# Three held weight tiles over half of the feature blocks at a time, turned tiles in side banks, turned one tile sooner

## The chip, the cores and the metric

The kernel runs on one core of one Trainium2 chip. The metric is the device time of one execution in microseconds; the time before is the median of three runs. TensorE multiplies, ScalarE (ACT) casts and copies, VectorE (DVE) subtracts, adds and scales, and SyncE (SP) and GpSimd (POOL) issue most of the transfers.

## The reference

512 tokens of width 1024 pass through two layers. Each layer is a feed-forward block, a mixer and another feed-forward block, each behind a norm and added to the stream; a final norm ends it.

```python
x = x + 0.5 * swiglu(rms_norm(x, ffn1_norm[l]), ffn1_wg[l], ffn1_wu[l], ffn1_wd[l])
h = rms_norm(x, mix_norm[l])
z = h @ w_in[l]                      # q | k | v | conv B | conv C | conv h
...                                  # window attention, and B * causal conv3(C * h)
x = x + jnp.concatenate([attn_out, conv_out], axis=-1) @ w_out[l]
x = x + 0.5 * swiglu(rms_norm(x, ffn2_norm[l]), ffn2_wg[l], ffn2_wu[l], ffn2_wd[l])
```

`swiglu(h)` is `(silu(h @ w_gate) * (h @ w_up)) @ w_down` with 2816 hidden features; `rms_norm` divides each token by its root mean square and multiplies by a gain. All is float32.

## The kernel before

**Numbers in two parts.** A float32 operand is split into a high part, a cast by ScalarE (`wh`, L204), and a low part, the rest, by VectorE (`wl`, L205). Each product is three matmuls: high by high, high by low and low by high. Weights go through three buffers for high parts and three for low parts. `need_split(g)` makes the splits up to number g; a split waits until the matmuls on the tile that held its buffer are done.

**Large blocks.** Most of the feed-forward work runs in a seven-product scheme on forms of the activations: b11, b21, b22 and the sums t1 to t4, kept as `fb` and `ft` tiles. Their low parts too are subtractions of L205.

**The stage behind a norm.** The stream is kept with tokens on the partitions (four tiles t of 128 tokens, two halves o of 512 features). When two token tiles are complete, `Norm.stage` makes their factors (L569 to L571, and the Newton step at L452 to L454) and the normed tiles `xn` (L577). `Norm.pull` takes one token half and one feature half: `turn` transposes two `xn` tiles on TensorE (L601, four transposes of 128x128 each) into a PSUM tile `xt`, ScalarE casts it (L610), VectorE subtracts (L611), and in front of a feed-forward block ScalarE copies it once more in full (`hf`, L613), from which the sums are made (L634 to L640). A norm has four pulls: two for the first 256 tokens, two for the second. PSUM has eight banks: four with tag "mm", two "sc" and two "aux"; `Norm.tags` says which the turned tiles take.

**The block that opens behind the norm** is `halves` (five times in the kernel, called A to E in order of time, at 348, 512, 851, 1192 and 1356 us of the profiled span: A and D in front of the mixers, B, C and E in front of feed-forward blocks). It holds three weight tiles of 1024 x 128, and runs the first 256 tokens (`t` 0) for one tile after the other over all eight feature blocks `k`, then the second 256 tokens. The third and the fourth pull lie between, behind the second tile and in the middle of the third:

```python
for t in range(2):
    for j, (hi, lo) in enumerate(held):
        for k in range(KC):
            ...                                        # three matmuls of 256 columns (L317)
            if t == 0 and (j, k) in ((1, KC - 1), (2, KC // 2 - 1)):
                norm.pull()
        if t:
            need_split(first + j + 3)
            done(j, accs[j])
```

`done` is the caller's: in `plain_halves` it starts the gate (silu, L940) or the product with the third tile and makes the sums t2, t3 and t1. There a fourth tile (`up`, L952) follows, then the seven-product stages (L837); in the mixer a plain `group` (L291 to L294) follows.

**What runs ahead of it.** At A, B and E it is `share` (L837, evictions at L871), as the out projection or as the last shared stage of a feed-forward block: its seventh product has the first two pulls between its matmuls. At C and D it is `down` (L340, evictions at L1149): for its second half it holds three weight tiles, finishes token tiles 0 and 1 first, and then runs the three weights over token tiles 2 and 3; the pulls stand behind the last weight's matmuls of tile 2 and of tile 3.

**Order.** From the second half of `down`, or the fifth step of `share`, to the end of `halves`, TensorE's instructions stand in the order of the program (`by_hand`). VectorE's, ScalarE's and the rest are put in order by a scheduler when the kernel is built, from what depends on what.

Of the kernel before, what the change touches and what calls it, by code (L numbers as in the profile page):

```python
# [23 lines left out]
KC = D // P  # L24
# [3 lines left out]
H = S // 2  # L28
# [44 lines left out]
def trunk_kernel(  # L73
# [23 lines left out]
    nc = tc.nc  # L97
# [8 lines left out]
    def psum(tag, shape, name):  # L106
        return ps.tile(shape, F32, tag=tag, bufs={"mm": 4, "sc": 2, "aux": 2}[tag], name=name)
# [94 lines left out]

    def split(hi, lo, raw, eng=nc.vector):
        nc.scalar.copy(hi, raw)  # L204
        eng.tensor_sub(lo, raw, f32(hi))  # L205

    def split_far(hi, lo, raw):

        nc.scalar.activation(lo, raw, AF.Copy, scale=-1.0)
        nc.scalar.copy(hi, raw)  # L210
        return nc.gpsimd.dma_start(out=f32(lo), in_=raw, accum_op=ALU.add)

    def need_split(g):
        while state["split"] <= min(g, len(order) - 1):
            n = state["split"]
            u, what = order[n]
            far = what == "far"
            if what in (None, "wide", "far"):
                need_raw(u if far else u + LOAD_AHEAD)
                raw = raw_of.pop(u)  # L220
            elif isinstance(what, tuple):

                what, h, how = what
                far = how == "far"
                last = {"a11": 0, "a12": 4, "s2": 2, "s3": 6, "s1": 2, "a22": 8, "s4": 4}[what]
                need_raw(u + h if far else u + max(last, 4) + h + LOAD_AHEAD)
                a11, s1, a12, s3, a22 = (raw_of.get(u + 2 * i + h) for i in range(5))
                if what == "s2":
                    late = state["late"] if h else None
                    with tc.issue_after(late) if late else nullcontext():  # L230
                        nc.vector.tensor_add(a11, a11, s1)  # L231
                raw = {"a11": a11, "a12": a12, "s2": a11, "s3": s3, "s1": s1, "a22": a22, "s4": a12}[what]
            else:

                need_raw(u + 4 + LOAD_AHEAD)
                a11, a12, s1, s3, a22 = (raw_of.get(u + i) for i in range(5))
                if what == "s2":
                    nc.vector.tensor_add(a11, a11, s1)
                if what == "s4":
                    nc.vector.tensor_add(a11, a11, a12)  # L240
                raw = {"a11": a11, "a12": a12, "s2": a11, "s3": s3, "s1": s1, "a22": a22, "s4": a11}[what]
                if what == FORMS[-1]:
                    for i in range(5):
                        del raw_of[u + i]
            shape = list(raw.shape)
            hi = wpool.tile(shape, F32R, tag="wh", bufs=3, name=f"wh_{n}")
            lo = wpool.tile(shape, F32R, tag="wl", bufs=3, name=f"wl_{n}")
            if far:
                sent = split_far(hi, lo, raw)
            else:  # L250
                split(hi, lo, raw)
            if isinstance(order[n][1], tuple):
                early = how == "early"
# [12 lines left out]
                for i in done:  # L266
                    del raw_of[u + 2 * i + h]
            split_of[n] = (hi, lo)
            state["split"] += 1
            if far:  # L270

                with tc.issue_after(sent.ins):
                    need_raw(u + LOAD_AHEAD + (4 + h if isinstance(order[n][1], tuple) else 0))

    def take_split(ahead=SPLIT_AHEAD):
        n = state["group"]
        state["group"] += 1
        need_split(n + ahead)
        return n, *split_of.pop(n)
# [27 lines left out]
    def halves(norm, n, done):  # L307

        first = state["group"]
        held = [take_split(SPLIT_AHEAD - j)[1:] for j in range(n)]  # L310
        accs = [psum("mm", [P, S], f"acc_{first + j}") for j in range(n)]
        for t in range(2):
            for j, (hi, lo) in enumerate(held):
                for k in range(KC):
                    xh, xl = norm.half(k, t)
                    for i, (w, x_) in enumerate(((hi, xh), (hi, xl), (lo, xh))):
                        nc.tensor.matmul(  # L317
                            accs[j][:, t * H : (t + 1) * H],
                            w[:, k, :],
                            x_,  # L320
                            start=t + k + i == 0,
                            stop=k == KC - 1 and i == 2,
                            skip_group_check=True,
                        )
                    if t == 0 and (j, k) in ((1, KC - 1), (2, KC // 2 - 1)):
                        norm.pull()
                if t:
                    need_split(first + j + 3)
                    done(j, accs[j])

    def down(acts, blocks, norm=None):

        last = len(blocks) - 1

        def products(acc, t, i, wh, wl):
            tok = slice(t * P, (t + 1) * P)
            ah, al = acts[blocks[i]]
            for k in range(2):
                for n, (a, w) in enumerate(((ah, wh), (al, wh), (ah, wl))):
                    nc.tensor.matmul(  # L340
                        acc,
                        a[:, k, tok],
                        w[:, k, :],
                        start=i + k + n == 0,
                        stop=i == last and k == 1 and n == 2,
                    )

        for o in range(2):
            accs = [psum("mm", [P, S], f"down_{state['group']}_{t}") for t in range(NT)]
            if o and norm:  # L350
                by_hand()
            if o and last:
                held = [take_split(SPLIT_AHEAD - i)[1:] for i in range(last + 1)]
                ahead = state["group"]
                for t in range(2):
                    for i, w in enumerate(held):
                        products(accs[t], t, i, *w)
                    yield t, o, accs[t]
                for i, w in enumerate(held):
                    for t in range(2, NT):  # L360
                        products(accs[t], t, i, *w)
                        if i == last:
                            yield t, o, accs[t]
                            if norm:
                                norm.pull()
                    need_split(ahead + i)
                continue
            for i in range(last + 1):
                _, wh, wl = take_split()
                for t in range(NT):  # L370
                    products(accs[t], t, i, wh, wl)
                    if i == last:
                        yield t, o, accs[t]
# [283 lines left out]
    norm = First()  # L657
# [52 lines left out]
    def squares(n):  # L710
# [756 lines left out]
    def stages_of(i):  # L1467
        mixing = i % 3 == 1
        gain = (ffn1_norm, mix_norm, ffn2_norm)[i % 3][i // 3]
        late = ("sc", "sc", "aux", "aux") if mixing else ("mm", "mm", "sc", "sc")  # L1470
        return Norm(i, gain, mixing, ("aux", "aux", "sc", "sc") + late)

    for l in range(DEPTH):
        n1, n2 = stages_of(3 * l + 1), stages_of(3 * l + 2)
# [4 lines left out]
        norm = n3  # L1479
# [30 lines left out]
```

## Time and profile before

| | us |
|---|---|
| median of three runs | 1699.25 (1699.24 to 1699.68) |
| profiled execution | 1701.48 |
| its span | 1699.7 |
| TensorE busy | 1679.4 (99%) |
| VectorE busy | 1323.5 (78%) |
| ScalarE busy | 953.2 (56%) |
| mean granted TensorE clock | 0.996 |

The profiled execution has its own time: its span runs from the first to the last instruction, and 1.8 us lie around it. A timeline row has the start, the duration, the engine, the line, the operation, output <- inputs, the sizes and a count; in brackets stands how long the engine had been idle before it, and who released it. Durations of matmuls overlap, so that their starts, not their durations, tell the pace. A row of the windows has the stretch, busy time and instructions of each engine, the granted clock, the share of DMA time and GB/s.

### The profile page before, as it was taken

The numbers are of one execution on the slowest core, as the hardware profiler recorded it, in microseconds if no ns is written. First come the engines' busy times: TensorE is split into PE (matmuls) and PEld (weight loads), VectorE is DVE, ScalarE is ACT, GpSimd is POOL, SyncE is SP. The second block draws the span as 40 slices with busy tenths as digits, with TensorE's granted clock in tenths as the row PEclk, the third lists the DMA queues.
The fourth block names the chain that finished last, engine by engine and source line by source line (L and its number), as shares of the span: only waits on it lengthen the run. The fifth ranks groups of instructions, "written<-read, shape, count | busy, mean of one in ns | idle before, by whom it ended". The sixth has DMA issues, their size and how long they took to land.

```text
span 1699.7 us, 21898 instructions
## 1 busy us (share of the span) xinstructions
PE 1679.4 (99%) x8222; PEld 1412.8 (83%) x8222; DVE 1323.5 (78%) x1734; ACT 953.2 (56%) x1361; POOL 182.2 (11%) x164
## 2 busy tenths in 40 slices
PE   9999999999999999999999999999999999999998
PEld 6888898888888888888888888888888888888887
DVE  6987679867798766899577668995587986668993
ACT  6455565556566555555455555553565765556553
POOL 0011111000110111111001111110001101111101
PEclk9999999999999999999999999999999999999999
DMA  9367788721494777788537777883225947777971
GB/s 248 87 186 187 185 194 213 191 73 57 132 221 103 203 180 185 185 223 221 128 73 200 184 186 185 224 214 109 63 61 143 224 113 192 178 186 185 233 185 50
DMA packets 189310, 279.85 MB, mean 165 GB/s; under 512 B 8948, under 2 KB 73492, under 8 KB 189204
## 3 DMA queue, kind: packets, MB, share of 16 engines
q1 hardware_dynamic: 150900, 203.34, 38.5%
q0 software_dynamic: 37600, 74.46, 26.2%
q8 instruction: 64, 1.05, 0.2%
q10 hardware_dynamic: 704, 0.66, 0.1%
q14 instruction: 42, 0.34, 0.1%
HBM read 263.74 MB, written 2.10 MB: 156 GB/s over the span
## 4 chain that ended last, share of the span: by engine, by line
PE 94%; DVE 4%; ACT 1%; issue 0%; DMA 0%; SPq 0%; DVEq 0%; ACTq 0%
PE x L837 24%; PE y L837 12%; PE x_s L837 10%; PE w L837 6%; PE down L340 6%; PE y_s L837 5%; PE acc L317 4%; PE acc L291 4%; PE acc L292 4%; PE acc L294 4%; PE w_s L837 3%; PE at L1077 2%; PE x_m L837 2%; DVE wl L205 1%; PE up L952 1%; PE acc L735 1%
## 5 line engine op out<-in xcount | busy, mean ns | idle before, releaser
L204 ACT CAST wh<-raw 128x1024 fp32r<-128x1024 f32 (+1 forms) x494 | 516.3, 1046 | 563.4 <-PE x L837 126.4
L205 DVE TENSOR_TENSOR wl<-raw,wh 128x1024 fp32r<-128x1024 f32 (+1 forms) x494 | 597.6, 1212 | 243.0 <-ACT wh L204 241.2
L837 PE MATMUL x<-wh,ft 128*128 128x512 f32 x608 | 188.6, 391 | 0.0
L837 PE MATMUL y<-wh,ft 128*128 128x512 f32 x608 | 188.4, 391 | 0.0
L837 PE MATMUL x<-wh,fb 128*128 128x512 f32 x608 | 187.1, 389 | 0.0
L837 PEld LDWEIGHTS x<-wh,fb 128*128 128x128 f32 x608 | 113.9, 188 | 23.4
L837 PEld LDWEIGHTS x<-wh,ft 128*128 128x128 f32 x608 | 113.1, 188 | 22.8
L837 PEld LDWEIGHTS y<-wh,ft 128*128 128x128 f32 x608 | 113.1, 188 | 22.7
L837 PE MATMUL x<-wl,ft 128*128 128x512 f32 x304 | 118.3, 389 | 0.0
L837 PE MATMUL y<-wl,ft 128*128 128x512 f32 x304 | 118.3, 389 | 0.0
L837 PE MATMUL x<-wl,fb 128*128 128x512 f32 x304 | 118.3, 389 | 0.0
L199 POOL DMA_DIRECT2D raw<-in_ffn_wu_dram x39 | 47.2, 1210 | 539.6 <-DMA raw<-in_ffn_wu_dram 407.5
L837 PE MATMUL w<-wh,fb 128*128 128x512 f32 x304 | 95.2, 394 | 0.0
L291 PE MATMUL acc<-hh,wh 128*128 128x512 f32 x240 | 94.6, 394 | 0.0
L294 PE MATMUL acc<-hh,wl 128*128 128x512 f32 x240 | 93.9, 391 | 0.0
L292 PE MATMUL acc<-hl,wh 128*128 128x512 f32 x240 | 93.6, 390 | 0.0
L340 PE MATMUL down<-wh,a 128*128 128x512 f32 x288 | 89.2, 391 | 0.0
L837 PE MATMUL y_s<-wh,ft_s 128*128 128x512 f32 x256 | 79.5, 392 | 0.0
L837 PE MATMUL x_s<-wh,ft_s 128*128 128x512 f32 x256 | 79.2, 390 | 0.0
L199 POOL DMA_DIRECT2D raw<-in_ffn_wg_dram x39 | 47.0, 1213 | 265.6 <-DMA raw<-in_ffn_wu_dram 97.5
L837 PE MATMUL x_s<-wh,fb_s 128*128 128x512 f32 x240 | 74.2, 390 | 0.0
L231 DVE TENSOR_TENSOR raw<-raw,raw 128x1024 f32<-128x1024 f32 x58 | 70.5, 1219 | 0.5
(320 smaller groups left out, 3439.8 us busy)
## 6 DMA issues: line engine op xcount, KB each, us to landing
raw<-in_ffn_wu_dram SPq DMA_DIRECT2D x126, 512.0 KB, 3.8
raw<-in_ffn_wd_dram SPq DMA_DIRECT2D x104, 512.0 KB, 5.1
raw<-in_ffn_wg_dram SPq DMA_DIRECT2D x86, 512.0 KB, 5.0
raw<-in_ffn_wu_dram POOLq DMA_DIRECT2D x39, 512.0 KB, 7.5
raw<-in_ffn_wg_dram POOLq DMA_DIRECT2D x39, 512.0 KB, 6.0
raw<-in_w_in_dram SPq DMA_DIRECT2D x36, 512.0 KB, 3.9
raw<-in_ffn_wd_dram POOLq DMA_DIRECT2D x32, 512.0 KB, 7.8
raw<-raw POOLq DMA_DIRECT2D x20, 512.0 KB, 6.9
```

The source lines that it names most:

```text
L199: nc.gpsimd.dma_start(out=r, in_=rows_of(*more), accum_op=ALU.add)
L204: nc.scalar.copy(hi, raw)
L205: eng.tensor_sub(lo, raw, f32(hi))
L231: nc.vector.tensor_add(a11, a11, s1)
L291: nc.tensor.matmul(acc, hi[:, k, :], rhs[k][0], start=k == first, stop=False)
L292: nc.tensor.matmul(acc, hi[:, k, :], rhs[k][1], start=False, stop=False)
L294: nc.tensor.matmul(acc, lo[:, k, :], rhs[k][0], start=False, stop=k == last)
L317: nc.tensor.matmul(accs[j][:, t * H : (t + 1) * H], w[:, k, :], x_, start=t + k + i == 0, stop=k == KC - 1 and i == 2, skip_group_check=True,)
L340: nc.tensor.matmul(acc, a[:, k, tok], w[:, k, :], start=i + k + n == 0, stop=i == last and k == 1 and n == 2,)
L735: nc.tensor.matmul(opening[n], (lo if part == "w" else hi)[:, k, :], xl if part == "x" else xh, start=n not in begun, stop=k == KC - 1 and ...
L837: nc.tensor.matmul(accs[u], x_[:, 2 * h + k, tok], w[:, k, :], start=start and h + k + i == 0, stop=h + k == 2 and i == 2, skip_group_chec ...
L1077: nc.tensor.transpose(tp[:, t * P : (t + 1) * P], ups[t][:, c * P : (c + 1) * P], ident)
```

## The change

Three edits. `halves` takes the feature blocks in two fours: for each token half, the three held tiles run over the first four blocks, then all three over the other four; the third and the fourth pull stand behind the first and the second tile of the second four. `need_split` and `done` are called behind a tile's last four blocks. In `down`, the two pulls move from behind the last of the three weights to behind the last but one. And the turned tiles of the second token half take the side banks, "aux", "aux", "sc", "sc", as those of the first do, instead of "mm", "mm", "sc", "sc" (in front of a feed-forward block) or "sc", "sc", "aux", "aux" (in front of a mixer).

```diff
@@ halves @@
         for t in range(2):
-            for j, (hi, lo) in enumerate(held):
-                for k in range(KC):
-                    xh, xl = norm.half(k, t)
-                    for i, (w, x_) in enumerate(((hi, xh), (hi, xl), (lo, xh))):
-                        nc.tensor.matmul(
...
-                    if t == 0 and (j, k) in ((1, KC - 1), (2, KC // 2 - 1)):
+            for half in range(2):
+                for j, (hi, lo) in enumerate(held):
+                    for k in range(KC // 2 * half, KC // 2 * (half + 1)):
+                        xh, xl = norm.half(k, t)
+                        for i, (w, x_) in enumerate(((hi, xh), (hi, xl), (lo, xh))):
+                            nc.tensor.matmul(
...
+                    if not t and half and j < 2:
                         norm.pull()
-                if t:
-                    need_split(first + j + 3)
-                    done(j, accs[j])
+                    if t and half:
+                        need_split(first + j + 3)
+                        done(j, accs[j])
@@ down @@
                         if i == last:
                             yield t, o, accs[t]
-                            if norm:
-                                norm.pull()
+                        if norm and i + 1 == last:
+                            norm.pull()
@@ stages_of @@
-        late = ("sc", "sc", "aux", "aux") if mixing else ("mm", "mm", "sc", "sc")
-        return Norm(i, gain, mixing, ("aux", "aux", "sc", "sc") + late)
+        return Norm(i, gain, mixing, ("aux", "aux", "sc", "sc") * 2)
```

The changed program has the same matmuls, casts and subtractions; on TensorE they stand in the written order, and the scheduler's order of ScalarE and VectorE changes around C and D and behind each `halves`.

More of the change, by code (lines that the diff above doesn't have):

```diff
@@ L312, in halves @@
         for t in range(2):
-            for j, (hi, lo) in enumerate(held):
-                for k in range(KC):
-                    xh, xl = norm.half(k, t)
-                    for i, (w, x_) in enumerate(((hi, xh), (hi, xl), (lo, xh))):
[L317 to L324, printed above, removed]
-                    if t == 0 and (j, k) in ((1, KC - 1), (2, KC // 2 - 1)):
+            for half in range(2):
[4 more added lines that the diff above has]
+                            nc.tensor.matmul(
+                                accs[j][:, t * H : (t + 1) * H],
+                                w[:, k, :],
+                                x_,
+                                start=t + k + i == 0,
+                                stop=k == KC - 1 and i == 2,
+                                skip_group_check=True,
+                            )
+                    if not t and half and j < 2:
                         norm.pull()
-                if t:
-                    need_split(first + j + 3)
-                    done(j, accs[j])
+                    if t and half:
+                        need_split(first + j + 3)
+                        done(j, accs[j])
     def down(acts, blocks, norm=None):
```

## The prediction

> **What bounds the kernel now.** I read the page first, then TensorE's waits, then the chain, the timelines and the windows around the five places where a norm ends and `halves` begins.
>
> ```profile
> PE 1679.4 (99%) x8222; PEld 1412.8 (83%) x8222; DVE 1323.5 (78%) x1734; ACT 953.2 (56%) x1361; POOL 182.2 (11%) x164
> ...
> PE 94%; DVE 4%; ACT 1%; issue 0%; DMA 0%; SPq 0%; DVEq 0%; ACTq 0%
> ```
>
> ```profile
> PE acc L317 <- ACT hf L613: 5.4, 3, 1.9
> ```
>
> TensorE is busy for 99% of the span and carries 94% of the chain. Time can come only from its stops and from stretches in which it runs slowly. Its longest wait in total, 5.4 us in three stops, is at L317, the matmuls of `halves`; the timelines below show more there and at L601, the turning transposes. So I measure each `halves` from its first matmul to the first matmul behind it. The starts and the stops inside, from the TensorE timeline (A and D lead into the mixers, B and E into the second feed-forward of a layer, C into layer 1):
>
> ```profile
> 348.33 0.28 PE L317 MATMUL acc<-hh,wh 128*128 128x256 f32 x1
> ...
> 354.52 1.29 PE L601 MATMUL xt<-ident,xn 128*128 128x128 f32 x8 [0.28 <-DVE xn L577]
> ...
> 368.02 0.40 PE L291 MATMUL acc<-hh,wh 128*128 128x512 f32 x1
> ...
> 511.67 0.40 PE L317 MATMUL acc<-fb,wh 128*128 128x256 f32 x2
> ...
> 520.98 0.80 PE L317 MATMUL acc<-fb,wh 128*128 128x256 f32 x2 [1.89 <-ACT hf L613]
> ...
> 534.84 0.40 PE L952 MATMUL up<-fb,wh 128*128 128x256 f32 x2
> ...
> 850.89 0.48 PE L317 MATMUL acc<-fb,wh 128*128 128x256 f32 x2
> ...
> 854.11 0.39 PE L317 MATMUL acc<-fb,wh 128*128 128x256 f32 x1 [1.55 <-ACT fb L610]
> ...
> 854.91 0.39 PE L317 MATMUL acc<-fb,wh 128*128 128x256 f32 x1 [0.41 <-DVE fb L611]
> ...
> 863.32 0.50 PE L317 MATMUL acc<-fb,wh 128*128 128x256 f32 x2 [1.58 <-ACT hf L613]
> ...
> 875.79 0.40 PE L952 MATMUL up<-fb,wh 128*128 128x256 f32 x2
> ...
> 1191.84 0.36 PE L317 MATMUL acc<-hh,wh 128*128 128x256 f32 x1
> ...
> 1193.91 0.39 PE L317 MATMUL acc<-hh,wh 128*128 128x256 f32 x1 [0.40 <-ACT hh L610]
> ...
> 1195.01 0.39 PE L317 MATMUL acc<-hl,wh 128*128 128x256 f32 x1 [0.70 <-DVE hl L611]
> ...
> 1212.54 0.40 PE L291 MATMUL acc<-hh,wh 128*128 128x512 f32 x1
> ...
> 1356.16 0.40 PE L317 MATMUL acc<-fb,wh 128*128 128x256 f32 x2
> ...
> 1365.48 0.50 PE L317 MATMUL acc<-fb,wh 128*128 128x256 f32 x2 [1.88 <-ACT hf L613]
> ...
> 1377.95 0.40 PE L952 MATMUL up<-fb,wh 128*128 128x256 f32 x2
> ```
>
> The five take A 19.69, B 23.17, C 24.90, D 20.70 and E 21.79 us. What they would take without a stop follows from two rows of the chain:
>
> ```profile
> 1367.17 0.87 PE xt L601 x8
> 1368.04 10.07 PE acc L317 x84
> ```
>
> 84 matmuls in 10.07 us are 0.12 each, and a pull (eight transposes) is 0.87. One `halves` is 144 matmuls and two pulls: 17.28 + 1.74 = 19.02. So A loses 0.67, B 4.15, C 5.88, D 1.68, E 2.77, together 15.15 us. That is the most that the change can bring.
>
> B and E issue the same work and differ by 1.38. The windows say why:
>
> ```profile
> 522.00:523.00 1.00, 1.00 (x6) 1.00 (x6) 0.00 (x0) 0.00 (x0) 0.52 (x1) 0.50 0.00 0
> ```
>
> ```profile
> 856.00:857.00 1.00, 1.00 (x6) 1.00 (x6) 1.00 (x2) 0.00 (x0) 0.00 (x0) 0.50 0.13 47
> ```
>
> In B and C the granted clock (third number from the end) is at 0.50 behind the stop. E's stop is as long, yet its 84 matmuls above ran at the full pace.
>
> **The change part by part.**
>
> *Banks (tags).* In B, C and E the third pull's tiles took "mm" banks, and the third accumulator could start only when ScalarE's full copy of a turned tile (hf) had freed one. With four side banks, and the third accumulator begun before that pull, this wait (1.89, 1.58, 1.88) goes. The side banks' former tiles were copied out long before. What would be late next is the pull itself, behind the norm's xn; that is costed below.
>
> *Turned sooner.* In C and D the pulls stand six matmuls of 512 columns earlier each. The first then starts twelve such matmuls ahead of its old place:
>
> ```profile
> 844.63 2.07 DVE L577 SCALAR_TENSOR_TENSOR xn<-x,y,gain 128x512 f32<-128x512 f32 x3
> ```
>
> ```profile
> 847.84 1.03 PE L601 MATMUL xt<-ident,xn 128*128 128x128 f32 x8
> ```
>
> ```profile
> 881.71 5.47 PE x L837 x24
> ```
>
> Old place 847.84; twelve matmuls of 512 columns (24 take 5.47) sooner is 845.1. The first xn is done at 844.63 and the second at 845.32, 0.2 before its own four transposes: no stop. The same instructions lie between here and `halves`, so its start stays. The casts and splits that these pulls feed come sooner on ScalarE and VectorE.
>
> *Feature blocks in two fours.* In C and D the second pull's block was needed twelve matmuls (1.44 us) into `halves`; now thirty-six (4.32 us). C's waits of 1.55 and 0.41 and D's of 0.40 and 0.70 go. The third and fourth pulls keep their places, behind 48 and 60 matmuls, but before the block that they feed is read there are now 24 matmuls and more, so no wait arises there.
>
> What the new order asks for sooner is the weights. The second held tile is read after 12 matmuls instead of 24, the third after 24 instead of 48, and each low part is wanted with its tile's third matmul. In A, B and E VectorE makes these parts late, in an order that the changed program keeps instruction for instruction:
>
> ```profile
> 512.33 1.21 DVE L205 TENSOR_TENSOR wl<-raw,wh 128x1024 fp32r<-128x1024 f32 x1
> ...
> 514.66 1.21 DVE L205 TENSOR_TENSOR wl<-raw,wh 128x1024 fp32r<-128x1024 f32 x1
> ...
> 516.97 2.74 DVE L577 SCALAR_TENSOR_TENSOR xn<-x,y,gain 128x512 f32<-128x512 f32 x4
> ```
>
> ```profile
> L317 PEld LDWEIGHTS acc<-fb,wl x144: 187/192/331, 511.8 to 1377.7; 128*128 128x128 f32 x144
> ```
>
> In B the second tile's low part is done at 513.54 and wanted at 511.67 + 14 x 0.12 = 513.35; the third's is done at 515.87 and wanted at 514.79. These are stationary operands, so a late one also shows its load, 0.19: the third tile's third matmul starts at 515.87 + 0.04 + 0.19 = 516.10, against 514.79. Both new waits together put TensorE back by 1.31. Queued behind are all of TensorE's later matmuls and both pulls; VectorE's xn does not wait for them. The block ends at 517.30, twelve more matmuls at 518.74, and by then the xn of the third pull (516.97 + 1.37) are ready, so the old stop at L601 (0.28 in A) goes. A and E show the same rows at the same distances: 1.31 each. With the low parts in time this is 0; if the second's own wait, 0.42, were not made up inside the third's, it is 1.73.
>
> In C and D the third tile's low part was done at 853.07 and 1193.55:
>
> ```profile
> 851.84 1.23 DVE L205 TENSOR_TENSOR wl<-raw,wh 128x1024 fp32r<-128x1024 f32 x1 [0.48 <-ACT wh L204]
> ```
>
> ```profile
> 1192.32 1.23 DVE L205 TENSOR_TENSOR wl<-raw,wh 128x1024 fp32r<-128x1024 f32 x1
> ```
>
> Wanted are 854.01 and 1194.96. In C the changed order puts the second pull's two subtractions ahead of it, so I get 853.6, just in time: 0, at most 0.3.
>
> *The end of `halves`.* `done` and `need_split` move: the first held tile's buffers come free 24 matmuls before the fourth tile is read, not 48. In B, C and E the changed order of VectorE has three subtractions of forms (ft2, ft3, t4) ahead of the fourth tile's low part, where none stood.
>
> ```profile
> 864.85 1.04 PE L601 MATMUL xt<-ident,xn 128*128 128x128 f32 x8
> ```
>
> ```profile
> 868.04 1.23 DVE L634 TENSOR_TENSOR sums<-hf,hf 128x1024 f32<-128x1024 f32 x1 [0.65 <-ACT hf L613]
> 869.30 1.22 DVE L636 TENSOR_TENSOR sums<-sums,hf 128x1024 f32<-128x1024 f32 x1
> 870.45 1.22 DVE L638 TENSOR_TENSOR hf<-hf 128x1024 f32<-128x1024 f32 x1
> 871.58 1.22 DVE L205 TENSOR_TENSOR wl<-raw,wh 128x1024 fp32r<-128x1024 f32 x1
> ```
>
> Call X the start of the second token half: last pull + 0.87 + 1.44. The sums begin 3.19 behind the pull, X + 0.88; three operations as shown (871.58 - 868.04 = 3.54) and three more at 1.14, the distance of those starts, bring the low part to X + 7.84; done X + 9.06, loaded X + 9.29. Wanted: X + 74 x 0.12 = X + 8.88. A wait of 0.40 in each of B, C and E (0 to 1.3, one more operation). In A and D no forms stand there, and the split, a cast and a subtraction, fits in the 24 matmuls' 2.88:
>
> ```profile
> L204 ACT CAST wh<-raw 128x1024 fp32r<-128x1024 f32 (+1 forms) x494 | 516.3, 1046 | 563.4 <-PE x L837 126.4
> ```
>
> 1.05 and 1.22 are 2.27. The loads on SP's and POOL's queues keep their order.
>
> *The clock.* No new stop reaches 1.55 (in A, B and E 0.42 and 0.89), the shorter of the two after which the trace shows the fall, so I cost the clock at full. The Trainium skill, "TensorE: Matmul & The Clock Gate" (Part 1), has the gate follow a free-running window of about 3.4 us, and its closing table allows gaps of up to about 3 us. By it the new waits cost no clock either and the sum is the same; but the trace fell at gaps of 1.89 and of 1.55 + 0.41, so its limit does not hold here unless the transposes ahead of B's gap count as idle, as its Part 4 suggests: then B's gap runs from 511.67 + 48 x 0.12 = 517.43 to 520.98.
>
> *Sum*, new minus old: A 19.02 + 1.31 - 19.69 = +0.64; B 19.02 + 1.71 - 23.17 = -2.44; C 19.02 + 0.40 - 24.90 = -5.48; D -1.68; E 19.02 + 1.71 - 21.79 = -1.06. Together -10.0. The profiled execution took 1701.48 us (span 1699.7, 1.8 around it): it would take 1691.5. The median of the runs, 1699.25, lies 2.2 lower, and with the same saving comes to 1689.2.
>
> **The rivals.**
>
> *No new waits* (0.06). If the scheduler's order let the low parts through sooner, all 15.15 come: 1684.1. Against it: in B VectorE's rows run from 512.33 to 515.87 without a gap.
>
> *The runs had a full clock* (0.17). A stretch at half clock is worth 1.38 (B against E). If the timed runs lacked both B's and C's, which the 2.2 between profile and median would allow, there is 2.8 less to win: 1692.0. For it: E, with B's stop, kept its pace. Against: the three runs agree within 0.44. The Trainium skill's free-running window (same page, Part 1) speaks for it too; no run so far shows it.
>
> *It doesn't take the early waits away* (0.06). If ScalarE's new order, casts of the turned tiles between casts of weights, makes the second pull late again, C's 1.96 and its slow stretch, 1.38, and D's 1.10 stay: 4.4 less, 1693.6.
>
> *The clock falls everywhere* (0.02 slower, 0.03 the same). In A, B and E `halves` now has two stops and two pulls in some 10 us. If at each of the five places the stops, and again the pulls, brought a stretch at half clock, ten at 1.38 would be 13.8 against the 10.0: 1703.0, slower. From five stretches on the gain is lost in the measurement, from ten on the kernel is slower. Against it: A, with a stop and two pulls close together, loses only 0.67 in all.
>
> **How the numbers follow.** The sum has 0.66. About 3.4 us (0.2%) can be told from no change; the sum and the first three rivals lie beyond that, so faster is 0.95, the same 0.03, slower 0.02. The sum's unknowns (A, B, E 0 to 1.73 each, the end 0 to 1.3 each, C 0.3) spread it over about 1686 to 1692; the range goes from 1686.0 to 1693.5, with the full-clock rival in it, and leaves 0.17 out.
>
> **What would show it.** In the changed trace: no wait of L317 on hf, nor on the second pull's casts in C and D; new waits of L317 on DVE wl L205 in A, B and E, near 0.3 and 0.9; one of L952 on wl near 0.4; A longer than before, C shorter by over 5; a clock of 1.00 in all five. Wrong would be: L317 waits on wl above 2 us, waits for the third or fourth pull's casts at the start of the second token half, a clock of 0.50 in more than two places, or new stops at L837 behind the plain block.

## The result

| | before | changed kernel |
|---|---|---|
| median of four runs, us | 1699.24 (1697.75 to 1699.68) | 1689.47 (1689.45 to 1689.48) |
| profiled execution, us | 1701.48 | 1689.48 |
| its span, us | 1699.7 | 1687.7 |

The ratio is 0.9944 (95% interval 0.9927 to 0.9961): faster by 9.8 us (0.6%), clear of the noise, against a forecast of 1689.2 in a range of 1686.0 to 1693.5.

In the changed kernel all lines behind L316 are one further down: L318 is `halves`, L602 the turning transposes, L953 the fourth tile (`up`). All waits of its TensorE, from the view of waits (total, times, longest):

```profile
PE acc L318 <- DVE wl L205: 1.9, 3, 0.6
PE x_m L838 <- DVE wl L205: 1.6, 2, 0.8
PE idle L140 <- DVE warm L682: 1.2, 1, 1.2
PE up L953 <- DVE wl L205: 0.9, 3, 0.4
PE xt L701 <- DMA x<-in_x_dram: 0.3, 1, 0.3
```

There is no wait for hf, fb, hh, hl or xn left. In their place stand waits for low parts of weights at two lines, L318 and `up`; those at L838, L140 and L701 lie elsewhere and stood in the trace of before too. The windows of the five stages, A to E, each from the first matmul of `halves` to the first behind it (stretch and length, TensorE busy, granted clock, DMA share, GB/s), first of before, then of the changed kernel:

```profile
348.33:368.02 19.69, 19.38 (x162) 1.00 0.36 104
511.67:534.84 23.17, 21.08 (x162) 0.93 0.58 143
850.89:875.79 24.90, 21.36 (x164) 0.93 0.34 84
1191.84:1212.54 20.70, 19.59 (x164) 1.00 0.28 80
1356.16:1377.95 21.79, 19.70 (x162) 1.00 0.62 154
```

```profile
345.97:366.21 20.24, 19.50 (x161) 1.00 0.25 74
509.87:530.11 20.24, 19.49 (x161) 1.00 0.58 134
846.79:865.79 19.00, 19.00 (x162) 1.00 0.36 84
1182.54:1201.53 18.99, 18.99 (x161) 1.00 0.20 57
1345.17:1365.41 20.24, 19.49 (x161) 1.00 0.59 141
```

C and D now run without a stop, at the 19.0 that the prediction worked out for that. A, B and E take 1.25 more than that, all three alike, and the clock is full everywhere. Where the 1.25 goes, from B's timelines of VectorE and TensorE:

```profile
510.54 1.21 DVE L205 TENSOR_TENSOR wl<-raw,wh 128x1024 fp32r<-128x1024 f32 x1
511.67 1.28 DVE L872 SCALAR_TENSOR_TENSOR x<-z_m,x 128x512 f32<-128x512 f32 x2
512.87 1.22 DVE L205 TENSOR_TENSOR wl<-raw,wh 128x1024 fp32r<-128x1024 f32 x1
```

```profile
511.81 0.38 PE L318 MATMUL acc<-fb,wl 128*128 128x256 f32 x1
...
514.14 0.38 PE L318 MATMUL acc<-fb,wl 128*128 128x256 f32 x1 [0.65 <-DVE wl L205]
...
530.11 0.40 PE L953 MATMUL up<-fb,wh 128*128 128x256 f32 x2
530.79 0.39 PE L953 MATMUL up<-fb,wl 128*128 128x256 f32 x1 [0.28 <-DVE wl L205]
```

The second tile's low part is done at 511.75 and the third's at 514.09; their first products start at 511.81 and 514.14. At 0.12 a matmul from 509.87 they would stand at 511.55 and 512.99, so they are 0.26 and 1.15 late, and the last 0.10 of the 1.25 is lost behind the second of them. With two matmuls of 0.12 behind 530.11 the low product of `up` would stand at 530.35; it stands at 530.79, 0.44 later, though the row shows an idle time of 0.28 alone. Between the stages, from the windows' ends and starts, the way from B to C grew by 0.63 us, from C to D by 0.70 and from E to the end by 0.54; those from A to B and D to E stayed within 0.02. That is 1.87 in all. Most of it is the wait at `up` with what hangs on it: in fours in the first half alone (below), which has no such wait, the same three ways are 0.10, 0.10 and 0.05 longer than before, so that 0.53, 0.60 and 0.49 are left for the wait.

So the five stages give 110.25 - 98.71 = 11.54 us, and 1.87 goes back behind them. The profiled executions differ by 12.0. The rest is the opening: A starts at 345.97 in place of 348.33, 2.36 sooner, and no edit of the change lies before A's first two pulls; the second profile of before, below, starts A at 346.07.

### The profile page after: what moved, and what is told of

The parts are those of the page before. It is cut to its first block, busy times and chain, and to the rows that moved or that the text cites. A ratio compares the mean times of both kernels' runs of the same rounds, so it can differ in the third digit from the quotient of the medians.

```text
span 1687.7 us, 21919 instructions
## 1 busy us (share of the span) xinstructions
PE 1674.4 (99%) x8222; PEld 1408.9 (83%) x8222; DVE 1324.7 (78%) x1734; ACT 953.4 (56%) x1361; POOL 182.3 (11%) x164
## 3 DMA queue, kind: packets, MB, share of 16 engines
q8 instruction: 64, 1.05, 0.2%
## 4 chain that ended last, share of the span: by engine, by line
PE 92%; DVE 6%; ACT 1%; issue 1%; DMA 0%; SPq 0%; DVEq 0%; ACTq 0%
PE x L838 25%; PE y L838 12%; PE x_s L838 10%; PE w L838 6%; PE down L341 5%; PE y_s L838 5%; PE acc L291 4%; PE acc L292 4%; PE acc L294 4%; PE w_s L838 3%; PE acc L318 2%; PE at L1078 2%; DVE wl L205 2%; PE x_m L838 1%; PE up L953 1%; PE acc L736 1%
## 5 line engine op out<-in xcount | busy, mean ns | idle before, releaser
L838 PE MATMUL x<-wh,ft 128*128 128x512 f32 x608 | 188.7, 391 | 0.0
L838 PE MATMUL y<-wh,ft 128*128 128x512 f32 x608 | 188.4, 391 | 0.0
L838 PE MATMUL x<-wh,fb 128*128 128x512 f32 x608 | 187.2, 389 | 0.0
L838 PEld LDWEIGHTS x<-wh,fb 128*128 128x128 f32 x608 | 113.9, 188 | 23.5
L838 PEld LDWEIGHTS x<-wh,ft 128*128 128x128 f32 x608 | 113.1, 188 | 22.8
L838 PEld LDWEIGHTS y<-wh,ft 128*128 128x128 f32 x608 | 113.1, 188 | 22.7
L838 PE MATMUL x<-wl,ft 128*128 128x512 f32 x304 | 118.3, 389 | 0.0
L838 PE MATMUL y<-wl,ft 128*128 128x512 f32 x304 | 118.3, 389 | 0.0
L838 PE MATMUL x<-wl,fb 128*128 128x512 f32 x304 | 118.3, 389 | 0.0
L838 PE MATMUL w<-wh,fb 128*128 128x512 f32 x304 | 95.2, 394 | 0.0
L838 PE MATMUL y_s<-wh,ft_s 128*128 128x512 f32 x256 | 79.5, 392 | 0.0
L838 PE MATMUL x_s<-wh,ft_s 128*128 128x512 f32 x256 | 79.1, 390 | 0.0
L838 PE MATMUL x_s<-wh,fb_s 128*128 128x512 f32 x240 | 74.2, 390 | 0.0
```

The source lines that it names most:

```text
L838: nc.tensor.matmul(accs[u], x_[:, 2 * h + k, tok], w[:, k, :], start=start and h + k + i == 0, stop=h + k == 2 and i == 2, skip_group_chec ...
```

## The experiments

The medians in the table are of the timed runs; A to E are the stages of each profiled execution. Beside banks only, banks and sooner turn, banks and order and order only the kernel before took 1698.97 us in the median of 15 runs, beside the others 1699.44 and 1699.40.

| kernel | median, us | A | B | C | D | E |
|---|---|---|---|---|---|---|
| before | 1699.24 | 19.69 | 23.17 | 24.90 | 20.70 | 21.79 |
| before, profiled again | 1697.92 (one run) | 19.71 | 21.80 | 24.90 | 20.71 | 21.78 |
| banks only | 1691.75 | 19.71 | 19.70 | 23.04 | 20.70 | 19.71 |
| sooner turn only | 1694.32 | 19.72 | 21.80 | 20.92 | 18.99 | 23.37 |
| order in fours only | 1697.21 | 20.24 | 24.03 | 21.33 | 19.08 | 22.47 |
| banks and order | 1689.24 | 20.23 | 20.24 | 19.07 | 19.07 | 20.23 |
| banks and sooner turn | 1686.17 | 19.69 | 19.69 | 18.99 | 18.99 | 19.72 |
| the whole change | 1689.47 | 20.24 | 20.24 | 19.00 | 18.99 | 20.24 |
| fours in the first half alone | 1688.15 | 20.25 | 20.25 | 18.99 | 18.99 | 20.26 |
| low parts late | 1686.48 | 19.78 | 19.77 | 19.00 | 18.99 | 19.78 |
| low parts between | 1686.57 | 19.72 | 19.71 | 18.99 | 18.99 | 19.72 |
| banks, sooner turn, later pull | 1684.24 | 19.01 | 19.00 | 19.01 | 19.00 | 19.00 |

### The three parts of the change

**Banks only**: of the diff, only the edit in `stages_of`.

> The kernel before with only the bank change: every plain block's late turned tiles go to the four side banks; the order of the held tiles and the pull in `down` are as before. Theory (each stop costs what its row shows, and the stops are apart from each other): the waits of TensorE for hf inside `halves` go, 1.89 in B, 1.58 in C, 1.88 in E, and with them the slow stretches behind them (1.38 in B). The early waits of C and D (1.55 + 0.41, 0.40 + 0.70) stay. A and D 0, B -3.7, C -1.8, E -2.3: -7.8, so some 1691.4 beside 1699.2 of the kernel before. No wait of a product for the low part of a held tile (wl) inside `halves`. Rival (the banks only move the stop: with the old order the turned tiles are copied by a VectorE that is still busy, so TensorE waits for the copies instead): under 3 us gained, 1696 or more, with waits for hf of like size left at the same places.

Measured: 1691.75 us (1691.71 to 1692.27), ratio 0.996 (0.9946 to 0.9973). Its waits inside `halves` and at the pulls:

```profile
PE acc L317 <- ACT fb L610: 1.6, 1, 1.6
PE xt L601 <- DVE xn L577: 0.9, 3, 0.3
PE acc L317 <- DVE hl L611: 0.7, 1, 0.7
PE acc L317 <- DVE fb L611: 0.4, 1, 0.4
PE acc L317 <- ACT hh L610: 0.4, 1, 0.4
```

All hf waits are gone, and the early ones of C and D stand untouched. B and E come to A's 19.7, with the pull's wait for xn, 0.29 in each, which stands in the trace of before too (0.28, 0.19 and 0.20). The banks are worth 7.2 us (1698.97 - 1691.75), against 7.8 expected, and no new wait stands in the stop's place. C keeps its slow stretch, a clock of 0.93 in its window:

```profile
845.02:868.06 23.04, 21.08 (x163) 0.93 0.36 86
```

**Banks and sooner turn**: the diff without the edit in `halves`.

> The whole change but for the order in fours: side banks, and the sooner turned tile in `down`, with each held tile run over all eight feature blocks as before. Theory (the order in fours takes away only waits that the other two parts take away too, and itself costs the waits for low parts: 1.2 in each of A, B and E in the profile of the changed kernel, and 0.3 for `up` in each of B, C and E): A as before at 19.7, B near 19.5, C and D near 19.0 to 19.3, E near 19.5, no wait of `halves` or `up` for wl. Sum some -13.6 from the kernel before: 1685.6, that is 3.8 under the 1689.5 of the changed kernel. Rival (the order in fours is what makes the early waits of C and D go, since a pulled tile is turned sooner but its copy still ends late): C keeps 1.96 and D 1.10 of wait and C its slow stretch, so about 4.5 more than the theory says: 1690, no better than the changed kernel.

Measured: 1686.17 us (1686.12 to 1686.56), ratio 0.9926 (0.9914 to 0.9939): 3.3 us faster than the whole change. Of its TensorE's waits only this one lies in the five stages; the others are at L700, L837 and L140:

```profile
PE xt L601 <- DVE xn L577: 0.9, 3, 0.3
```

C and D run clean at 18.99, and no wait for wl stands in `halves` or at `up`, as the theory had it; it had B and E at 19.5, and they take 19.7. So the order in fours adds no gain to the other two parts, and costs.

**Banks and order**: the diff without the edit in `down`.

> The changed kernel without the sooner turned tile in `down`: side banks and the order in fours. Theory (the order in fours alone puts the first use of the last turned blocks some 24 products, 2.9 us, later, more than the 1.55 + 0.41 that C waited): C and D keep at most 0.3 us of waits, the time is 1689.5 to 1690.0, no different from the changed kernel. Rival (the sooner turn is what takes the early waits away, the order does not): C keeps 1.96 and its slow stretch and D keeps 1.10, some 1693.5 to 1694, 4 us above the changed kernel.

Measured: 1689.24 us (1689.13 to 1689.83), ratio 0.9944 (0.9932 to 0.9957), level with the whole change. C and D show no wait here either, at 19.07. The early waits go by the sooner turn alone and by the order alone; together they take off no more than the 0.08 between 19.07 and 18.99.

**Order in fours only**: the edit in `halves` alone.

> The kernel before with only the order in fours: old banks for the late turned tiles, old place of the pull in `down`. Theory (with the old banks the third pull's tiles share a bank tag with three open sums, so one of its turned tiles waits for a copy of the other, about 2 us, and the waits for low parts come on top): A +0.55, B -0.5, C -3.5, D -1.7, E +0.9: -4.3, some 1695. Rival (the order in fours alone is enough, since it lets the stop of the old banks fall where TensorE has other products): within 1 us of the changed kernel, 1689 to 1690.5. Rival the other way (the order in fours with old banks brings the weight waits and leaves all else): 1701 to 1703, slower than before.

Measured: 1697.21 us (1695.78 to 1699.96), ratio 0.9993 (0.9984 to 1.0001), 2.2 us above what the theory gave; the interval holds 1, so that no gain can be told here. The timeline shows the third pull in B, half of it before and half behind the copy that frees its bank:

```profile
516.49 0.60 PE L602 MATMUL xt<-ident,xn 128*128 128x128 f32 x4
...
519.11 0.77 PE L602 MATMUL xt<-ident,xn 128*128 128x128 f32 x4 [2.02 <-ACT hf L614]
```

With the old banks the new order moves the hf stop from the third sum to the second turned tile, and lengthens it to 2.02, in B, C and E. The mechanism came out as the theory had it. Its size was missed in two places. In this execution B, with a clock of 0.93, took 24.03 for E's 22.47. And the ways behind B, C and E are 0.4 longer each than in the second profile of before (849.97 - 533.53 = 316.44 from B to C, for 847.27 - 531.22 = 316.05). The list of waits has no row for `up`, but the starts show one there, behind 533.53 in B:

```profile
534.07 0.39 PE L953 MATMUL up<-fb,wl 128*128 128x256 f32 x1
534.29 0.40 PE L953 MATMUL up<-fb,wh 128*128 128x256 f32 x2
```

Without a wait these would stand at 533.77 and 533.89; they are 0.30 and 0.40 late. VectorE ends the low part at 534.01.

**Sooner turn only**: the edit in `down` alone.

> The kernel before with only the sooner turned tile in `down`: old banks, old order of the held tiles. Theory (the early waits of C and D belong to the late turn alone, and the hf stops of B, C and E to the banks alone, so the parts add): D falls to 19.0 as in the run of banks and sooner turn; C loses what the run of banks only and that of banks and sooner turn differ by, 23.0 - 19.0 = 4.0, and keeps its hf stop of 1.6 to 1.9; B and E keep theirs. Sum -4.0 - 1.7 = -5.7 from the kernel before: 1693 to 1693.5, with the spread of some microseconds that the two kernels with hf stops show. Rival (the hf stop of C is set by the same late copies and grows once the early waits are gone): C only to 22 or more, 1695 or more.

Measured: 1694.32 us (1693.85 to 1695.43), ratio 0.997 (0.9959 to 0.9982). The stops are apart: C 24.90 - 20.92 = 3.98 and D 1.71 less, as expected, with the hf stops left at 1.89, 1.66 and 1.89. The median is 0.8 above the expectation's upper end. In before's first profile the slow one of B and E was B; here it is E, by 1.57 (23.37 - 21.80; the window of E):

```profile
1347.50:1370.87 23.37, 21.28 (x161) 0.93 0.58 145
```

Between A and B this execution waits 1.43 us for a low part at L837, where before waited 0.77. Which of the two the timed runs have, and so what the 0.8 is, no trace shows.

### What the order in fours costs

**Fours in the first half alone**: the changed kernel, with the old order in the second token half.

```diff
         for t in range(2):
-            for half in range(2):
+            size = (KC, KC // 2)[t == 0]
+            for k0 in range(0, KC, size):
                 for j, (hi, lo) in enumerate(held):
-                    for k in range(KC // 2 * half, KC // 2 * (half + 1)):
+                    for k in range(k0, k0 + size):
...
-                    if not t and half and j < 2:
+                    if not t and k0 and j < 2:
                         norm.pull()
-                    if t and half:
+                    if t:
                         need_split(first + j + 3)
                         done(j, accs[j])
```

> The changed kernel, but with the fours only in the first token half; in the second each held tile runs over all eight blocks as before. Theory (the waits of `up` for the low part of the fourth tile come from the fours in the second token half, since the first held tile's weights are let go 2.9 us before the end of the stage and not 5.8): the three waits at the `up` line go, that is 0.44 + 0.51 + 0.44 by the starts of the rows; A, B and E stay at 20.2. 1689.5 - 1.4 = 1688.1. Rival (the form subtractions ahead of the fourth tile's split on VectorE make that wait, as the prediction had it): they stay, 1689.2 to 1689.7.

Measured: 1688.15 us (1687.86 to 1688.44), ratio 0.9934 (0.992 to 0.9948). The waits at `up` are gone and A, B, E are unchanged. The expectation set two causes against each other that are one chain, as ScalarE's and VectorE's timelines at B's end show, first of the changed kernel, where B ends at 530.11, then of this one, where it ends at 530.72:

```profile
526.10 2.36 DVE L205 TENSOR_TENSOR ft<-sums,ft 128x1024 fp32r<-128x1024 f32 x2
527.31 1.06 ACT L204 CAST wh<-raw 128x1024 fp32r<-128x1024 f32 x1 [0.29 <-PE acc L318]
528.38 1.22 DVE L641 TENSOR_TENSOR sums<-sums,hf 128x1024 f32<-128x1024 f32 x1
529.52 1.22 DVE L205 TENSOR_TENSOR wl<-raw,wh 128x1024 fp32r<-128x1024 f32 x1
```

```profile
525.04 1.05 ACT L204 CAST wh<-raw 128x1024 fp32r<-128x1024 f32 x1 [1.96 <-PE acc L319]
...
526.64 1.22 DVE L205 TENSOR_TENSOR wl<-raw,wh 128x1024 fp32r<-128x1024 f32 x1
...
528.97 1.23 DVE L205 TENSOR_TENSOR ft<-sums,ft 128x1024 fp32r<-128x1024 f32 x1 [1.10 <-ACT ft L204]
```

The fourth tile's cast waits for the first tile's last matmul. With the fours in the second half that matmul comes later: the cast starts 2.8 us ahead of B's end and not 5.7 (527.31 and 525.04), and three operations on the forms (526.10, two, and 528.38), which otherwise stand behind, come ahead of the split. That the late release brings the wait is shown by this run; that the operation at 528.38 holds the split up is read from the rows, where the split's subtraction follows it (529.52) though the cast is done at 528.37.

**Low parts late**: this kernel, with the low products of the first four blocks moved back.

In short, for its three tiles, with `a` the first four blocks and `b` the others (the second token half runs as in the kernel before):

```python
# run(tile, t, blocks, parts): parts 0 and 1 are the high part's products, 2 the low part's
for j in range(n):
    run(j, 0, a, (0, 1))
for j in range(2):
    run(j, 0, a, (2,))
for j in range(n):
    run(j, 0, b, (0, 1, 2))
    if j == 0:
        run(2, 0, a, (2,))
    if j < 2:
        norm.pull()
```

> The run before this in the list (fours only in the first token half), and with the products of the first four blocks with the low parts moved behind those with the high parts: high parts of three tiles, low parts of the first and second, the first tile's other four blocks, then the low part of the third. Theory (A, B and E are 1.25 longer than C and D only because the low parts of the second and third tile are not ready): no wait for wl in `halves`, A, B and E at 19.0, 1688.1 - 3.75 = 1684.3. Rival (the weights' splits end late however the products stand, so the wait moves to another product or the split gets later): A, B and E at 19.6 or more, 1686 to 1688.

Measured: 1686.48 us (1686.35 to 1688.06), ratio 0.9926 (0.9914 to 0.9939). The waits for wl are gone, yet A, B and E stand at 19.8, so that the theory's 1684.3 failed and the rival's time held, with another wait than it named. The timeline of A has the new wait:

```profile
347.68 1.29 DVE L884 SCALAR_TENSOR_TENSOR x<-z_s,x 128x512 f32<-128x512 f32 x2
...
348.51 0.36 PE L318 MATMUL acc<-hh,wh 128*128 128x256 f32 x1 [0.56 <-DVE x L884]
```

The third sum now begins after 16 matmuls, not 24. Its first matmul waits for the residual's addition (L884), which reads the last sum of `share` (`z_s`); that the two share a bank is what this wait points to.

**Low parts between**: the same, with the low parts of the first two tiles ahead of the third tile, whose sum so begins after 24 matmuls again.

> As the run with the low parts late, with another order of the first four blocks: high parts of the first and the second tile, low parts of the first and the second, then the high part of the third; its low part stays behind the first tile's other four blocks. Theory (that run lost 0.78 in A, B and E because the third sum began after 16 products in place of 24 and so met the residual's addition, L884 there, which frees its bank; 24 products in front of it are enough, as in the changed kernel): no wait in `halves`, A, B and E at 19.0, 1686.5 - 2.3 = 1684.2, level with the run of the later pull. Rival (with four blocks at a time there is no order in which neither the bank nor the low part is late): a wait of 0.3 or more stays in A, B and E, 1685 to 1686.5.

Measured: 1686.57 us (1686.05 to 1687.17), ratio 0.9928 (0.9915 to 0.9942). Neither bank nor low part is late, and A, B and E still take 19.7. What is late is the pull:

```profile
PE xt L612 <- DVE xn L588: 0.9, 3, 0.3
```

That is the wait for xn that before had in these stages and the whole change had not. The theory fell. The rival had its 0.3 of wait (0.29 and 0.30), though not where it put it, and its time to within 0.07. TensorE comes to the third pull after 48 matmuls in both orders. If nothing holds it up on the way it is there before xn is. In the changed kernel it had been held up by the low parts.

**Later pull**: banks and sooner turn, with the third pull two blocks later.

```diff
-                    if t == 0 and (j, k) in ((1, KC - 1), (2, KC // 2 - 1)):
+                    if t == 0 and (j, k) in ((2, 1), (2, KC // 2 - 1)):
```

> Side banks and sooner turn, old order, and inside `halves` the third pull two blocks later, behind block 1 of the third held tile in place of block 7 of the second; the fourth stays. Theory (the 0.28 wait of the turned tile for xn, which costs A, B and E 0.70 each against 18.99, is a matter of 0.4 us in the place of the pull): A, B and E at 19.0 to 19.1, 1686.2 - 2.1 = 1684.1. Rival (the two pulls now come so close that their casts and subtractions bunch up, and the second token half waits for them): a wait for hh, hl or fb of 0.3 to 1 us in A, B and E takes the gain back, 1685.5 to 1688.

Measured: 1684.24 us (1684.18 to 1685.86), ratio 0.9914 (0.99 to 0.9927). All five stages stand at 19.0, as the theory had it, and 5.2 us are gained on the whole change. The stages take 95.02 us together, 15.2 less than in the first profile of before: all that the prediction had called the most. All waits of its TensorE, none of them in the five:

```profile
PE x_m L837 <- DVE wl L205: 1.6, 2, 0.8
PE idle L140 <- DVE warm L681: 1.2, 1, 1.2
PE acc L735 <- ACT h L471: 0.2, 1, 0.2
```

It is the fastest of these kernels, with two of the three edits and one pull moved.

### Before, once more

> The kernel before, profiled once more. Theory (behind a stop of 1.6 to 2.0 the clock is at half for 1.4 us of products in some executions and not in others, whichever stage; and the opening takes 2.3 us more where the first weights land late): the parts outside the five stages and the opening agree with the first profile within 0.5 us; the slow stretches (B and C in the first profile) may lie in other stages, by 1.4 each; the opening up to the 48 products at L735 starts at 16.2 or at 18.5. Rival (slow stretches belong to B and C of this kernel, by what runs there): B and C at 23.2 and 24.9 again, E at 21.8.

Measured: 1697.92 us, 3.56 less than in the first profile. The opening's 48 matmuls in the chain of the first profile and of this one:

```profile
1.74 4.81 DMA raw<-in_ffn_wg_dram
...
18.55 11.06 PE acc L735 x48
```

```profile
1.75 4.08 DMA raw<-in_ffn_wg_dram
...
16.32 11.06 PE acc L735 x48
```

And the windows of B and C (E is at 21.78 with a full clock):

```profile
509.42:531.22 21.80, 19.70 (x161) 1.00 0.63 153
847.27:872.17 24.90, 21.35 (x164) 0.93 0.34 84
```

The opening is 2.23 sooner, and B lacks its slow stretch of 1.37: 3.60 together, against the 3.56. C has its own again. So the theory holds for B, whose slow stretch is not its own; C's came back in both profiles. Of the opening's 2.23 only 0.73 is the first weights' landing (4.81 for 4.08). The other 1.50 is a slow stretch there too: in the first profile the clock is at half from 8.66 to 12.08 us, in the second it is full. A window of the first:

```profile
10.00:11.00 1.00, 1.00 (x4) 0.50 1.02 387
```

## Why the prediction was right

**The hf stops.** The banks alone took them away, as the first step said. They cost more than their rows: B at full clock 21.80 - 19.70 = 2.10 for a row of 1.89, C 24.90 - 23.04 = 1.86 for 1.58. The prediction went by the length of the stages and not by the rows, which held.

**The early waits of C and D.** They are gone, by 4.05 (23.04 - 18.99) with the slow stretch in C and 1.71 in D. The prediction gave their removal to the order in fours (36 matmuls in place of 12) and costed the sooner turn as free. The order is enough by itself, as banks and order shows; but so is the sooner turn, as banks and sooner turn shows, and that one costs next to nothing (316.20 and 316.15 us from B to C and from C to D, for 316.04 and 316.05 in banks only). The prediction left that unsaid. It also said that each pull moves by six matmuls; both move by twelve (in banks and sooner turn they start 5.91 and 3.65 us ahead of C, in banks only 3.04 and 0.79).

**The low parts of the held tiles.** Forecast 1.31 in each of A, B and E, measured 1.25: the wait that was argued from VectorE's rows of before came, and within 0.06 of its size. Its row shows 0.65, and the second tile's wait has no row of its own, where 0.3 and 0.9 had been named as what the trace would show; by the starts in B they are 0.26 and 0.89. The load of 0.19 that the sum put ahead of a late product was put too high: the product starts 0.05 behind its low part, and 0.10 is lost behind it. The third pull's wait for xn went for the reason given, that TensorE comes later; low parts between showed it from the other side. So the low parts cost 0.55 net, as in the +0.64 for A.

**The fourth tile.** Forecast 0.40 in each of B, C and E, with the three form subtractions ahead of the split. Fours in the first half alone shows that the wait comes with the late release, and the rows show the forms ahead of the split as forecast; the size was short. By the starts the waits are 0.44, 0.51 and 0.44, and by the ways to the next stage 0.53, 0.60 and 0.49.

**C's third tile and the clock.** The low part was in time (C takes 19.00), and none of the waits, 0.65 at most by its row, brought the clock down: 1.00 in all five. The 1.55 from which this was argued was not the shortest stop with a fall behind it: before's opening fell behind one of 1.26 (at L700).

**The sum, with what comes behind each stage.** A +0.55 for +0.64, B -2.30 for -2.44, C -5.20 for -5.48, D -1.71 for -1.68, E -1.01 for -1.06: -9.67 for -10.0. The profiled execution fell by 2.3 more than that, to 1689.48 where the sum had 1691.5. The runs did not: before's first profile had a late opening, its median lies where an opening like that of the second puts it (1701.48 - 2.23 = 1699.25), and the prediction, which took the sum off the median, met it. In that there was luck: the prediction did not know what the 2.2 us were, and its sum counts B's slow stretch as won, which the second profile of before lacks; against a before of 1697.92 the same changed kernel gains 8.4.

**The rivals.** No new waits and the early waits staying are refuted by the waits above. The full clock in the timed runs is refuted for C: all three executions of C with early waits (before twice, banks only) had the clock at 0.93. For B and E it was half right: the second profile of before had neither slow. The 2.2 us between profile and median, on which that rival was built, fit the opening, two thirds of which is a slow stretch: the rival had a right cause in a wrong place. How many timed runs of before had a slow B or E no trace shows. The nine runs of before beside low parts between lie in two groups, three at 1697.37 to 1697.61 and six at 1699.30 to 1699.59; one stretch at half clock in B or E, 1.37 to 1.57, would make most of that step. The spread alone doesn't tell: the kernels with hf stops spread over 4.2 us (before, 15 runs), 4.2 (order only, 11) and 1.6 (sooner turn only, 6), those without over 0.03 (the whole change, 4) to 1.7 (later pull, 4, and low parts late, 5). The fall of the clock everywhere did not happen.

## What to carry to other kernels

A reordering that gives one operand more time takes it from another: before you reorder a loop over held tiles, list for each operand (activations, low parts, banks, the next tile's buffers) when it is ready and when the new order wants it first. Take the parts of a change singly: here the two edits that only moved an instruction or a buffer won 12.8 us (1698.97 - 1686.17), and the third gave 3.3 of it back for a wait that was already gone. Measure a stage from start to start, since a wait's row can show half of what it costs, and take off a wait only after you have named the one that was hidden behind it (low part, then bank, then xn).

## What the runs showed of the hardware

**The clock behind a stop.** Behind C's early waits (1.55 and 0.41 us, some 0.4 apart) the granted clock fell in three executions of three. Behind the stops of 1.58 to 2.02 it fell in 3 of 12: in B of before's first profile, in E of sooner turn only, in B of order only, and in none of the second profile's three. So the same stop, in the same program, costs 1.4 us more in one execution than in the other. A seventh fall is that in the opening of before's first profile. Other than these there are only those at the end of each execution, when TensorE has no work left.

By windows of 1 us each of the seven holds 3.40 to 3.42 us at half clock. And they lie on a grid: in before's first profile they start at 8.66, 520.66 and 855.18 us (a window of 1 us with a clock of 0.83 holds 0.34 us at half, so the fall at B starts at 520.66). That is 512.00 and 334.52 apart, 150 and 98 times 3.413. Cut into pieces on that grid, these are the windows with the stops of C, of B (and the piece behind it) and of E in that profile, then the two with B's stop in the second, whose grid is counted from C's fall at 852.34:

```profile
851.75:855.17 3.42, 1.46 (x10) 1.00 0.42 116
517.25:520.66 3.41, 1.64 (x11) 1.00 0.66 224
520.66:524.07 3.41, 3.09 (x14) 0.50 0.23 22
1363.75:1367.17 3.42, 1.69 (x14) 1.00 0.09 33
```

```profile
514.42:517.83 3.41, 2.23 (x16) 1.00 1.11 256
517.83:521.25 3.42, 2.51 (x21) 1.00 0.18 69
```

In the first profile B's stop lies whole in one piece, TensorE is idle for 1.77 of its 3.41 us, and the next piece runs at half clock. In the second an edge at 517.83 cuts the same stop into 1.18 and 0.91 idle, and nothing falls. In the five profiles with a fall ahead of the end, the pieces ahead of six falls were idle for 1.77 to 2.02 us, and every piece behind which the clock stayed for 1.73 or less. So behind the stops of `halves` it was not the length alone that decided, but where the stop lay on the grid. The seventh fall doesn't fit a mark drawn by idle time: the piece ahead of it in the opening (5.25 to 8.66) had 1.34 idle and 1.08 of transposes. What transposes count for stays open.

The Trainium skill, "TensorE: Matmul & The Clock Gate" (Part 1), says that the gate's window runs freely and doesn't reset when a kernel starts; the grid, which lies differently against B in the two profiles of before, agrees with that. Its closing table lets gaps of up to about 3 us pass without a fall; these falls came at stops of 1.9 and 2.0 and at two that are 1.96 together, so the limit does not hold here. Counting transposes as idle doesn't explain C: the piece ahead of its fall (851.75 to 855.17) has none.

**What a wait's row leaves out.** A stop cost 0.70 us where the turned tile waited 0.28 to 0.29 (A 19.71 in banks only, 19.01 with the later pull; in A of before the pull starts 0.44 late, and 1.05 lies between it and the next matmul where 0.79 lies at the fourth pull), 0.44 where `up` waited 0.28, and 1.25 in A, B and E of the changed kernel, where one row shows 0.63 to 0.65 and the second tile's wait, ahead of it, none. In order only, `up` was 0.40 late with no row at all.
